# Second half of the tokens laid out turned by the loader, scaled by roots spread over all partitions

## The chip, the cores and the metric

The kernel runs on one core of one Trainium2 chip. The metric is device time of the whole program in microseconds (us); lower is better. The core has a matrix engine (TensorE, PE in the profile), three elementwise engines (VectorE, DVE; ScalarE, ACT; GpSimd, POOL), and SyncE (SP), which here issues almost all DMAs. Every engine runs its own instructions strictly in the order in which they are written, and waits on semaphores for the others.

## The reference

One decoder layer over 2048 tokens of width 1024. The change lies in its first step, the norm and the combined projection:

```python
def rmsnorm(x, g):
    xf = x.astype(jnp.float32)
    y = xf * lax.rsqrt(jnp.mean(xf * xf, axis=-1, keepdims=True) + EPS)
    return (y * g.astype(jnp.float32)).astype(x.dtype)
...
    nx = rmsnorm(h, attn_norm_g[l])
    proj = jnp.einsum('bsd,dp->bsp', nx, w_in[l])
    gq, gk, gv, gr, glow, dq, dk_, dv_ = jnp.split(proj, split_at, axis=-1)
    ... two attention mixers on the pieces of proj, whose results are joined in `mixed` ...
    h = h + jnp.einsum('bsm,md->bsd', mixed, w_out[l])
    nm = rmsnorm(h, mlp_norm_g[l])
    a = jnp.square(jax.nn.relu(jnp.einsum('bsd,df->bsf', nm, w_ff1[l])))
    h = h + jnp.einsum('bsf,fd->bsd', a, w_ff2[l])
return rmsnorm(h, final_norm_g)
```

## The kernel before

**Numbers and products.** All matrix products are made from float32 values split in a rounded part ("hi") and the rest ("lo"): `mm3` (L131) issues three matmuls, hi·hi, lo·hi and hi·lo, into one PSUM bank. The large products are done by a Strassen-Winograd scheme with seven products in place of eight. So every operand has to exist on the chip as hi and lo: ACT makes the hi part by a copy, DVE the lo part by a subtraction.

**The projections** (L222 to L849) take x turned, features on the partitions and tokens along the row. Tokens 0 to 1023 are handled in a first pass (a product ahead of the groups, then groups g = 0 to 7), tokens 1024 to 2047 in a second (g = 8 to 16). For the second pass the kernel needs four blocks of the turned and normed x in SBUF: S11 and S21 (tokens 1024 to 1535, features 0 to 511 and 512 to 1023, in the buffers `xp` and `bp`), S12 and S22 (tokens 1536 to 2047, in two further buffers). S12 is held less S11. Before the change, `pair(i, step)` makes them while the first pass still runs: per i it loads two tiles of 128 tokens into the two halves of `acc[0]` (`x_load`, L553), squares and sums them on ACT with `xt` as the throw-away output (`square`, L571), takes the root (`root`: a tensor_scalar on DVE, L162, and a power on POOL, L163), scales by root and gain on DVE (`scale`, L577), turns them by eight TensorE transposes a tile (`turned`, L560), and moves the result out of PSUM: three copies on ACT (L603, L604, L607) and one subtraction on DVE (L608).

**What sets the order.** In this stage all five engines are ordered by hand. `on(t, f, ...)` files a step under a tick t; a loop (L837) runs through the ticks, emits a tick's steps in the order in which they were filed, and then one `product` of the running group. A narrow group (128 columns, g = 1 to 6) has 14 ticks of six matmuls with 512 columns; a wide one (g = 7 on) 28 ticks of twelve matmuls with 256 columns. Ticks below are counted from `base[0]`, the start of g = 0: g = 1 starts at tick 28, g = 2 at 42, g = 3 at 56, g = 4 at 70, g = 5 at 84, g = 6 at 98, g = 7 at 112. The products of a group are taken in the order j = 1, 2, 6, 5, 7, 4, 3; in a narrow group each has two ticks.

**What a narrow group does beside its products.** `hi` (ACT, L293) five ticks and `lo` (DVE, L298 or L300) three ticks ahead of their product, two in group 7; `wsum` (L305) sums of weight blocks; `evict` reads a bank two ticks after its product began: L364 (ACT) copies j = 1 into c11, L366 (ACT) copies j = 6 into c12, L368 (ACT) copies j = 7 into c21, and L370 and L373 (DVE) add. j = 1, 6 and 7 are summed in one bank, U, one upon the other, so j = 6 can't start before L364 has read it, nor j = 7 before L366 has. `finish_narrow` splits the four results (ACT L387, DVE L389) and stores them (SP L392, or L383 without a split): c11 at tick 7 of its group, c22 at tick 14, c21 at tick 15, c12 at tick 17, which is tick 3 of the next group. The next group's L364 and L366 overwrite c11 and c12 and have to wait for those stores.

**The bias rows.** `bias_rows` (ticks 46 to 52) makes three rows of 8x384 by small matmuls, copies them to `rbo`, whose third part lies in `xt`, and at tick 52 stores them to DRAM as `rowD` (L536).

Of the kernel before, what the change touches and what calls it, by code (L numbers as in the profile page):

```python
# [10 lines left out]
F32 = mybir.dt.float32  # L11
# [7 lines left out]
D = 1024  # L19
# [87 lines left out]
def emit(tc, a, stop=99):  # L107
# [8 lines left out]
    def ps(tag):  # L116
        return psum.tile([128, 512], F32, name="ps_" + tag, tag=tag, bufs=BANKS[tag])
# [5 lines left out]
    def view(t, shape):  # L123
        n = int(np.prod(shape))
        names = "abcd"[:len(shape)]
        return t[:, :n].rearrange(f"p ({' '.join(names)}) -> p {' '.join(names)}", **dict(zip(names, shape)))
# [19 lines left out]
    one = const.tile([1, 128], F32, name="one")  # L146
    V.memset(one, 1.0)
    gn = const.tile([128, 4], F32, name="gn")
    xt = const.tile([128, 1024], F32, name="xt")
    stats = const.tile([128, 96], F32, name="stats")  # L150
    stat_at = [0]
# [81 lines left out]
    def on(t, f, *args):  # L233
        ticks.setdefault(t, []).append((f, args))
# [284 lines left out]
                    on(B + t + dt, gate, g, k, step)  # L519

    rb, oh = bp[:33, :8], view(bp[:33, 8:], (3, 384))
    rbo = [bp[:8, 1160:1544], bp[:8, 1544:1928], xt[:8, :384]]

    def bias_load():
        SP.dma_start(rb[:32], a["rel_bias"])
# [26 lines left out]
    def x_load(t, dst):  # L552
        SP.dma_start(dst, token_rows(x2, t, D))  # L553

    def turned(xt):
        out = []
        for q in range(2):
            pv = view(ps("d"), (4, 128))
            for k in range(4):
                T.transpose(pv[:, k, :], xt[:, (4 * q + k) * 128:(4 * q + k + 1) * 128], ident)  # L560
            out.append(pv)
        return out

    def parts(j, i):
        return [v[:, :, i * 128:i * 128 + 128] for v in TB[j]]

# [2 lines left out]
    def square(key, src, junk):  # L569
        R[key] = stat()  # L570
        A.activation(junk, src, AF.Square, accum_out=R[key])  # L571

    def root(key):
        R[key] = rstd_of(R[key], D)

    def scale(key, src, cs=slice(0, D)):
        V.scalar_tensor_tensor(src[:, cs], src[:, cs], R[key], gB[:, cs], op0=OP.mult, op1=OP.mult)  # L577
# [4 lines left out]
    def blocks_12_22():  # L582
        if not later_blocks:
            later_blocks.update({n: view(slot(n), (4, 512)) for n in ("s12", "s22")})
        return later_blocks.values()


    def pair(i, step):

        at_ = slice(128 * i, 128 * i + 128)  # L590
        x = [acc[0][:, D * k:D * k + D] for k in range(2)]
        if step < 2:
            x_load(8 + i + 4 * step, x[step])
        elif step < 4:
            square((i, step - 2), x[step - 2], xt)
        elif step < 6:
            root((i, step - 4))
        elif step < 8:
            scale((i, step - 6), x[step - 6])
        elif step < 10:  # L600
            PV[0] = turned(x[step - 8])
        elif step == 10:
            A.activation(S11[:, :, at_], PV[0][0], AF.Copy)  # L603
            A.activation(S21[:, :, at_], PV[0][1], AF.Copy)  # L604
        else:
            S12, S22 = blocks_12_22()
            A.activation(S22[:, :, at_], PV[0][1], AF.Copy)  # L607
            V.tensor_tensor(S12[:, :, at_], PV[0][0], S11[:, :, at_], op=OP.subtract)  # L608

    for i in range(4):  # L610
        for step, dt in enumerate((0, 1, 5, 6, 6, 7, 8, 9, 10, 12, 11, 13)):
            on(base[0] + 51 + 18 * i + dt, pair, i, step)

    def half_sum(n, q):

# [117 lines left out]
    with tc.manual_schedule(engines={X.engine for X in (T, V, A, G, SP)}):  # L733
        A.dma_start(g_row, bass.AP(tensor=a["attn_norm_g"].tensor, offset=a["attn_norm_g"].offset, ap=[[D, 1], [1, D]]))
        x_load(0, xs[0])
        load_dv(0)
        x_load(1, xs[1])
        load_dv(1)
        load_dv(2)
        x_load(2, xs[2])  # L740
        load_dv(3)
        for t in range(3, 8):
            x_load(t, xs[t])
        SP.dma_start(w2b[:16], a["gla_gate_w2"].rearrange("o r k -> (o r) k"))
        SP.dma_start(w2b[16:17], a["gla_gate_b"])
        SP.dma_start(gn, bass.AP(tensor=a["gla_norm_g"].tensor, offset=a["gla_norm_g"].offset, ap=[[1, 128], [128, 4]]))
        V.memset(gT, 1.0)
        warm = open_bank()
        for _ in range(8):
            T.transpose(warm[:, :128], ident, ident)  # L750
        gb = [open_bank() for _ in range(2)]
        for q in range(2):
            T.matmul(gb[q], one, g_row[:, 512 * q:512 * q + 512], start=True, stop=True)
        square(0, xs[0], junk)
        V.tensor_copy(gB[:, :512], gb[0])
        root(0)
        V.tensor_copy(gB[:, 512:], gb[1])
        for cs in (slice(0, 512), slice(512, D)):
            scale(0, xs[0], cs)
        tile_T(0)  # L760
        hi_dv(0)
        lo_dv(0)
        square(1, xs[1], junk)
        tile_hi(0)
        tile_lo(0)
        root(1)
        hi_dv(1)
        tile_keep(0)
        dv_piece(0, 0)
        scale(1, xs[1])  # L770
        lo_dv(1)
        tile_T(1)
        dv_piece(0, 1)
        tile_hi(1)
        tile_lo(1)
        hi_dv(2)
        lo_dv(2)
        square(2, xs[2], junk)
        root(2)
        tile_keep(1)  # L780
        scale(2, xs[2])
        hi_dv(3)
        lo_dv(3)
        dv_piece(1, 0)
        dv_piece(1, 1)
        dv_piece(0, 2)
        dv_piece(1, 2)
        square(3, xs[3], junk)
        root(3)
        tile_T(2)  # L790
        tile_hi(2)
        tile_lo(2)
        tile_keep(2)
        scale(3, xs[3])
        dv_piece(0, 3)
        dv_piece(1, 3)
        square(4, xs[4], junk)
        for m in range(4):
            dv_piece(2, m)
            if m == 0:  # L800
                tile_T(3)
                dv_evict(0)
                dv_evict(1)
            if m == 1:
                tile_hi(3)
                tile_lo(3)
                root(4)
                dv_store(0)
                dv_store(1)
        tile_keep(3)  # L810
        scale(4, xs[4])
        for t in range(3, 8):
            n = t + 1
            on(4 * t, dv_evict, t - 1)
            on(4 * t + 2, dv_store, t - 1)
            if n < 8:
                on(4 * t + 1, tile_T, n)
                on(4 * t + 2, tile_hi, n)
                on(4 * t + 2, tile_lo, n)
                on(4 * t + 3, tile_keep, n)  # L820
                on(4 * t + 4, sums_G, n)
                for k, j in enumerate((5, 6)):
                    on(4 * t + 5, part_hi, j, n - 4, halves(n)[k])
                    on(4 * t + 6, part_lo, j, n - 4, halves(n)[k])
            if n < 7:
                on(4 * t + 1, square, n + 1, xs[n + 1], junk)
                on(4 * t + 2, root, n + 1)
                on(4 * t + 3, scale, n + 1, xs[n + 1])
            for m in range(4):
                on(4 * t + m, dv_piece, t, m)  # L830
        on(T0, dv_evict, 7)
        on(T0 + 2, dv_store, 7)
        for i in range(4):
            for k, j in ((0, 7), (1, 4)):
                on(T0 + 1 + 2 * i + k, part_hi, j, i, halves(i)[k])
                on(T0 + 2 + 2 * i + k, part_lo, j, i, halves(i)[k])
        for t in range(12, base[NG] + 10):  # L837
            ops = ticks.pop(t, [])
            for f, args in ops:
                if f is not dv_piece:  # L840
                    f(*args)
            for f, args in ops:
                if f is dv_piece:
                    f(*args)
            if T0 <= t < base[NG]:
                g = max(g for g in range(NG) if base[g] <= t)
                x, i = divmod(t - base[g], length[g])
                product(7 * g + x, i)
        assert not ticks, sorted(ticks)  # L849
# [993 lines left out]
def _order():  # L1843
    r, i = np.divmod(np.arange(128), 8)
    return 16 * i + r
# [28 lines left out]
def build(nc, inputs, stop=99):  # L1874
    arrays, aps = {}, {}
    for name in _INS:
        arrays[name] = np.ascontiguousarray(inputs[name])
    arrays.update(_constants())
    for name, v in arrays.items():
        aps[name] = nc.dram_tensor(name, v.shape, mybir.dt.from_np(v.dtype), kind="ExternalInput").ap()  # L1880
    aps["out"] = nc.dram_tensor("out", (1, S, D), F32, kind="ExternalOutput").ap()
    with tile.TileContext(nc, schedule_with_timeline_sim=True) as tc:
        emit(tc, aps, stop)
    return arrays
# [10 lines left out]
```

## Time and profile before

| | us |
|---|---|
| median of 3 timed runs | 2257.23 (2255.97 to 2259.64) |
| the profiled execution, whole | 2256.31 |
| its span, first to last instruction | 2254.5 |
| PE busy | 2229.1, 99% of the span |
| DVE busy | 1605.4, 71% |
| ACT busy | 1164.0, 52% |
| POOL busy | 812.5, 36% |
| granted TensorE clock | 0.998 |
| DMA, mean | 184 GB/s |

The span leaves out 1.8 us around the instructions. Busy time counts what an engine executes, not its waiting. A line of the timeline gives the start, the length, the engine, the source line and operation, output and inputs, shapes, and in brackets how long the engine sat idle before it and what ended that. An entry of the waits reads: who waited, for whom, us in total, times, longest. For DMAs, the time to landing runs from the issue to the completion that others can wait for.

### The profile page before, as it was taken

The page shows a single profiled execution, that of the slowest core. Times are in us where ns is not written, and L with a number is a line of the kernel's source. Part 1 is how long each engine was busy: PE and PEld are TensorE (multiplying, and loading weights), DVE is VectorE, ACT ScalarE, POOL GpSimd, SP SyncE. Part 2 cuts the span into 40 slices and gives each one's busy share as a digit, 9 for nine tenths or more (in the row PEclk, how much of TensorE's full clock was granted, in tenths as well). Part 3 has the DMA queues.
Part 4 walks back from the last instruction along what each step waited for, and adds up shares of the span by engine and source line. Part 5 has one row for each costly group of instructions (what it writes and reads, how often), then busy time and mean ns, then how long its engine had stood idle before and what let it go on. Part 6 is the DMA issues. An engine that isn't in the chain of part 4 may idle for free.

```text
span 2254.5 us, 34335 instructions
## 1 busy us (share of the span) xinstructions
PE 2229.1 (99%) x12324; PEld 1925.5 (85%) x12324; DVE 1605.4 (71%) x2757; ACT 1164.0 (52%) x2088; POOL 812.5 (36%) x802
## 2 busy tenths in 40 slices
PE   9999999999999999999999999999999999999998
PEld 7978998899999998888888887888888888888886
DVE  6866767746766784446677779777776878758897
ACT  6554446435777782234555557555563333323544
POOL 2111000005378766300122235232345645232665
PEclk9999999999999999999999999999999999999999
DMA  7256444757657864777344457444488653454563
GB/s 207 87 179 194 131 137 153 256 177 238 217 194 240 280 208 150 225 243 263 115 150 145 150 187 226 143 146 148 137 273 306 202 169 130 142 168 149 174 219 112
DMA packets 308267, 415.23 MB, mean 184 GB/s; under 512 B 19509, under 2 KB 236126, under 8 KB 302464
## 3 DMA queue, kind: packets, MB, share of 16 engines
q1 hardware_dynamic: 307950, 412.77, 57.1%
q8 instruction: 97, 1.59, 0.3%
q14 instruction: 74, 0.61, 0.1%
q10 hardware_dynamic: 146, 0.27, 0.0%
HBM read 268.48 MB, written 149.20 MB: 185 GB/s over the span
## 4 chain that ended last, share of the span: by engine, by line
PE 91%; DVE 4%; issue 2%; DMA 1%; ACT 1%; POOL 0%; SPq 0%; POOLq 0%; ACTq 0%; DVEq 0%
PE ps_a L132 11%; PE ps_a L133 11%; PE ps_a L134 11%; PE ps_c L132 9%; PE ps_c L134 8%; PE ps_c L133 8%; PE ps_a L1005 5%; PE ps_d L133 4%; PE ps_d L132 4%; PE ps_d L134 4%; PE ps_d L986 3%; PE ps_c L966 2%; PE ps_c L964 2%; PE ps_o L132 2%; PE ps_o L134 2%; PE ps_o L133 2%
## 5 line engine op out<-in xcount | busy, mean ns | idle before, releaser
L1442 ACT ACTIVATE w1comb<-w1raw 128x512 fp32r<-128x512 f32 x224 | 141.4, 633 | 243.3 <-PE ps_a L134 81.8
L1624 ACT ACTIVATE cs<-rs 128x1024 fp32r<-128x1024 f32 x104 | 109.7, 1055 | 218.7 <-PE ps_c L134 127.8
L1447 DVE TENSOR_TENSOR w1comb<-w1raw,w1comb 128x512 fp32r<-128x512 f32 x224 | 175.8, 786 | 27.5 <-ACT w1comb L1442 27.5
L977 ACT ACTIVATE pe<-pe,O 128x256 f32<-128x256 f32 (+1 forms) x384 | 156.2, 454 | 62.2 <-DVE O L976 57.6
L1005 PE MATMUL ps_a<-v,pt 128*128 128x65 f32 x1200 | 179.0, 252 | 0.0
L1005 PEld LDWEIGHTS ps_a<-v,pt 128*128 128x128 f32 x1200 | 173.4, 193 | 0.9
L986 PE MATMUL ps_d<-ident,pe 128*128 128x128 f32 x600 | 158.1, 278 | 0.0
L976 DVE CUSTOM_DVE_ANT_0 pe<-ps_c,nb 128x256 f32<-128x256 f32 (+1 forms) x384 | 126.7, 361 | 41.5 <-PE ps_d L986 16.8
L132 PE MATMUL ps_a<-hb,w1comb 128*128 128x512 f32 x384 | 149.7, 390 | 0.0
L133 PE MATMUL ps_a<-hb,w1comb 128*128 128x512 f32 x384 | 149.5, 389 | 0.0
L134 PE MATMUL ps_a<-hb,w1comb 128*128 128x512 f32 x384 | 149.4, 389 | 0.0
L1666 DVE TENSOR_TENSOR ct<-rt,ct 128x1024 fp32r<-128x1024 f32 x68 | 129.8, 1909 | 18.8 <-ACT ct L1662 18.8
L133 PE MATMUL ps_c<-ct,cs 128*128 128x512 f32 x360 | 140.1, 389 | 0.0
L132 PE MATMUL ps_c<-ct,cs 128*128 128x512 f32 x360 | 140.1, 389 | 0.0
L134 PE MATMUL ps_c<-ct,cs 128*128 128x512 f32 x360 | 140.1, 389 | 0.0
L163 POOL TENSOR_TENSOR stats<-stats,mhalf 128x1 f32<-128x1 f32 (+1 forms) x64 | 50.0, 783 | 242.6 <-DVE stats L162 242.5
L918 POOL CAST qp<-qs 128x512 fp32r<-128x512 f32 x64 | 66.6, 1126 | 180.2 <-DMA srD<-xp 164.1
L1547 POOL TENSOR_TENSOR acc<-acc 128x256 f32<-128x256 f32 x75 | 69.1, 931 | 160.9 <-DVE acc L1547 148.6
L1631 DVE SCALAR_TENSOR_TENSOR cs<-rs,cs 128x1024 fp32r<-128x1024 f32 (+1 forms) x56 | 100.0, 1793 | 29.6 <-ACT cs L1624 29.3
L293 ACT ACTIVATE wcomb<-wraw 128x512 fp32r<-128x512 f32 (+2 forms) x119 | 89.1, 756 | 60.2 <-DVE wraw L305 25.2
L1547 POOL TENSOR_TENSOR xt<-acc,acc 128x256 f32<-128x256 f32 x32 | 28.1, 878 | 226.7 <-ACT acc L1509 210.3
L986 PEld LDWEIGHTS ps_d<-ident,pe 128*128 128x128 f32 x600 | 108.0, 185 | 0.3
(434 smaller groups left out, 7319.4 us busy)
## 6 DMA issues: line engine op xcount, KB each, us to landing
rs<-actD SPq DMA_DIRECT2D x103, 512.0 KB, 3.7
actD<-acc SPq DMA_DIRECT2D x288, 128.0 KB, 2.9
w1raw<-w_ff SPq DMA_DIRECT2D x32, 1024.0 KB, 6.5
rt<-w_ff SPq DMA_DIRECT2D x24, 1024.0 KB, 7.2
k<-kD SPq DMA_DIRECT2D x16, 1024.0 KB, 8.5
rb<-hTD SPq DMA_DIRECT2D x13, 1024.0 KB, 7.6
wraw<-w_in SPq DMA_DIRECT2D x12, 1024.0 KB, 5.3
cmb<-boD SPq DMA_DIRECT2D x16, 528.0 KB, 6.2
```

What stands on the lines that cost most here:

```text
L132: T.matmul(out, sh, mh, start=first, stop=False, skip_group_check=more)
L133: T.matmul(out, sl, mh, start=False, stop=False, skip_group_check=more)
L134: T.matmul(out, sh, ml, start=False, stop=last, skip_group_check=more)
L976: V.tensor_tensor_reduce(p, s, bias, scale=1.0, scalar=BIG, op0=OP.add, op1=OP.min, accum_out=nm)
L977: A.activation(p, p, AF.Exp, bias=nm, scale=-1.0)
L986: T.transpose(pb[:, i * 128:i * 128 + 128], src, ident)
L1005: T.matmul(self.b.opsum[:, n % 4], self.pt[:, i * 128:i * 128 + 128], self.b.v[:, blk, cols], start=first, stop=last)
L1442: A.activation(c[:, 0], v, AF.Copy)
L1447: V.tensor_tensor(c[:, 1], v, c[:, 0].bitcast(F32), op=OP.subtract)
L1624: A.activation(v[:, 0], x, AF.Copy, scale=float(PRODUCTS[ph // 2][2]))
L1631: V.scalar_tensor_tensor(v[:, 1], x, -1.0, v[:, 0].bitcast(F32), op0=OP.mult, op1=OP.subtract)
L1666: V.tensor_tensor(v[:, 1], x, v[:, 0].bitcast(F32), op=OP.subtract)
```

## The change

The host lays out tokens 1024 to 2047 of x a second time, turned, as `x_turned` (features on 128 partitions by 8 by 1024 tokens). The four blocks S11, S21, S12 and S22 are loaded from it, 1 MB each, straight to their places (`load_turned`). The same tokens are still loaded as rows too, one tile every seven ticks (`tile_stats`), for their squares and roots alone. `spread_roots(k)` then makes a bank whose every partition holds the 512 roots of half k: four float32 matmuls, each with the root column of a tile repeated along 128 columns as the stationary operand and the identity as the moving one. `scale_turned` multiplies a 128x512 piece of a block in place by its gain (`gc`, a new constant of 128x8 loaded in the prologue) and by that bank; `less_first` takes S11 from S12. The third bias row moves from `xt` to `bp`.

```diff
+    gc = const.tile([128, 8], F32, name="gc")
...
-    rbo = [bp[:8, 1160:1544], bp[:8, 1544:1928], xt[:8, :384]]
+    rbo = [bp[:8, 1160:1544], bp[:8, 1544:1928], bp[:8, 8:392]]
...
-    def turned(xt):
-        out = []
-        for q in range(2):
-            pv = view(ps("d"), (4, 128))
-            for k in range(4):
-                T.transpose(pv[:, k, :], xt[:, (4 * q + k) * 128:(4 * q + k + 1) * 128], ident)
-            out.append(pv)
-        return out
...
-    def pair(i, step):
-
-        at_ = slice(128 * i, 128 * i + 128)
-        x = [acc[0][:, D * k:D * k + D] for k in range(2)]
-        if step < 2:
-            x_load(8 + i + 4 * step, x[step])
-        elif step < 4:
-            square((i, step - 2), x[step - 2], xt)
-        elif step < 6:
-            root((i, step - 4))
-        elif step < 8:
-            scale((i, step - 6), x[step - 6])
-        elif step < 10:
-            PV[0] = turned(x[step - 8])
-        elif step == 10:
-            A.activation(S11[:, :, at_], PV[0][0], AF.Copy)
-            A.activation(S21[:, :, at_], PV[0][1], AF.Copy)
-        else:
-            S12, S22 = blocks_12_22()
-            A.activation(S22[:, :, at_], PV[0][1], AF.Copy)
-            V.tensor_tensor(S12[:, :, at_], PV[0][0], S11[:, :, at_], op=OP.subtract)
-
-    for i in range(4):
-        for step, dt in enumerate((0, 1, 5, 6, 6, 7, 8, 9, 10, 12, 11, 13)):
-            on(base[0] + 51 + 18 * i + dt, pair, i, step)
+    def tile_stats(n, step):
+
+        x = acc[0][:, D * (n % 2):D * (n % 2) + D]
+        if step == 0:
+            x_load(8 + n, x)
+        elif step == 1:
+            square(8 + n, x, xt)
+        else:
+            root(8 + n)
+
+    rows = {}
+
+    def spread_roots(k):
+
+        rows[k] = ps("d")
+        for i in range(4):
+            T.matmul(rows[k][:, 128 * i:128 * i + 128], R[8 + 4 * k + i].to_broadcast([128, 128]), ident,
+                     start=True, stop=True)
+
+    def later_block(q, k):
+        return (S11, S21)[q] if k == 0 else list(blocks_12_22())[q]
+
+    def load_turned(q, k):
+        SP.dma_start(later_block(q, k), a["x_turned"][:, 4 * q:4 * q + 4, 512 * k:512 * k + 512])
+
+    def scale_turned(q, k, c):
+        v = later_block(q, k)[:, c]
+        V.scalar_tensor_tensor(v, v, gc[:, 4 * q + c:4 * q + c + 1], rows[k], op0=OP.mult, op1=OP.mult)
+
+    def less_first(c):
+        v = later_block(0, 1)[:, c]
+        V.tensor_tensor(v, v, S11[:, c], op=OP.subtract)
+
+    for n in range(8):
+        for step, dt in enumerate((0, 5, 6)):
+            on(base[0] + 51 + 7 * n + dt, tile_stats, n, step)
+    for k, t in ((0, 80), (1, 108)):
+        on(base[0] + t, spread_roots, k)
+        for q in range(2):
+            on(base[0] + (56, 90)[k] + 2 * q, load_turned, q, k)
+            for c in range(4):
+                on(base[0] + t + 1 + 4 * q + c, scale_turned, q, k, c)
+    for c in range(4):
+        on(base[0] + 110 + c, less_first, c)
...
+        SP.dma_start(gc, bass.AP(tensor=a["attn_norm_g"].tensor, offset=a["attn_norm_g"].offset, ap=[[1, 128], [128, 8]]))
...
+    later = np.asarray(inputs["x"]).reshape(NT, 128, CH, 128)[HT:, _order()]
+    arrays["x_turned"] = np.ascontiguousarray(later.transpose(3, 2, 0, 1).reshape(128, CH, 128 * HT))
```

Two places show how the change moves instructions. The first is SP's queue from tick 51 to tick 60, where group 2 (kD) ends and group 3 begins; before:

```order
L553 DMA acc_134<-x 128x1x1024
L271 DMA wraw_120<-w_in 128x8x256
L553 DMA acc_134<-x 128x1x1024
L536 DMA rowD_107<-bp_112 8x384 x2
L536 DMA rowD_107<-xt_77 8x384
L392 DMA kD1_89<-acc_135 256x1x512
L392 DMA kD1_89<-acc_136 256x1x512
L392 DMA kD0_88<-acc_136 256x1x512
L545 DMA rbD2_110<-rowD_107 128x2x384
```

and in the changed kernel, whose lines and buffer numbers stand one higher:

```order
L554 DMA acc_135<-x 128x1x1024
L272 DMA wraw_121<-w_in 128x8x256
L537 DMA rowD_108<-bp_113 8x384 x3
L393 DMA kD1_90<-acc_136 256x1x512
L603 DMA xp_112<-x_turned 128x4x512
L393 DMA kD1_90<-acc_137 256x1x512
L554 DMA acc_135<-x 128x1x1024
L603 DMA bp_113<-x_turned 128x4x512
L393 DMA kD0_89<-acc_137 256x1x512
L546 DMA rbD2_111<-rowD_108 128x2x384
```

The second row tile is now loaded behind two of the group's three stores instead of ahead of the bias rows, and two loads of 1 MB stand among the stores; the last of them, c12 (kD0 from acc_137), has 2.5 MB of loads in front of it.

The second place is DVE's queue from tick 108 to tick 117, where group 6 ends and the first weights of the wide group 7 are split (128x1024); before:

```order
L370 TENSOR_TENSOR acc<-ps_a,acc 128x512
L373 TENSOR_TENSOR acc<-ps_o,acc 128x512
L298 TENSOR_TENSOR wcomb<-wraw,wcomb 128x1024
L305 TENSOR_TENSOR wraw<-wraw 128x4x256
L162 TENSOR_SCALAR stats<-stats 128x1
L373 TENSOR_TENSOR acc<-ps_a,acc 128x512
L305 TENSOR_TENSOR wraw<-wraw 128x4x256
L162 TENSOR_SCALAR stats<-stats 128x1
L577 SCALAR_TENSOR_TENSOR acc<-acc,stats,misc 128x1024
L298 TENSOR_TENSOR wcomb<-wraw,wcomb 128x1024
```

and in the changed kernel, from the second row of these on (L374 is L373 there, L299 is L298, L306 is L305; s_1706 is the buffer of S12, s_1707 of S22):

```order
L374 TENSOR_TENSOR acc<-ps_o,acc 128x512
L299 TENSOR_TENSOR wcomb<-wraw,wcomb 128x1024
L607 SCALAR_TENSOR_TENSOR s_1706<-s_1706,gc,ps_d 128x512
L611 TENSOR_TENSOR s_1706<-s_1706,xp 128x512
L306 TENSOR_TENSOR wraw<-wraw 128x4x256
L607 SCALAR_TENSOR_TENSOR s_1706<-s_1706,gc,ps_d 128x512
L611 TENSOR_TENSOR s_1706<-s_1706,xp 128x512
L374 TENSOR_TENSOR acc<-ps_a,acc 128x512
L306 TENSOR_TENSOR wraw<-wraw 128x4x256
L607 SCALAR_TENSOR_TENSOR s_1706<-s_1706,gc,ps_d 128x512
L611 TENSOR_TENSOR s_1706<-s_1706,xp 128x512
L607 SCALAR_TENSOR_TENSOR s_1707<-s_1707,gc,ps_d 128x512
```

One more L611 follows, and then the second 128x1024 split. Between the eviction of ps_o and that split, two L162 and one L577 have gone, and four L607 and four L611 have come.

## The prediction

> **What bounds the kernel now.** First the page, its busy times and the chain of work that ended last:
>
> ```profile
> PE 2229.1 (99%) x12324; PEld 1925.5 (85%) x12324; DVE 1605.4 (71%) x2757; ACT 1164.0 (52%) x2088; POOL 812.5 (36%) x802
> PE 91%; DVE 4%; issue 2%; DMA 1%; ACT 1%; POOL 0%; SPq 0%; POOLq 0%; ACTq 0%; DVEq 0%
> ```
>
> PE is busy for 99% of the span and is 91% of the chain. So a PE instruction taken away is worth the time for which it holds up the next one, and any other work costs nothing until PE waits for it. The question is which waits PE has in the stage that changes, and which it will get. The waits from 140 to 260 us, the timeline of ACT and PE around the longest, and the merged chain there:
>
> ```profile
> ACT xt L571 <- DMA rowD<-xt: 4.5, 1, 4.5
> ...
> PE ps_a L132 <- ACT acc L364: 2.6, 1, 2.6
> ...
> PE ps_d L560 <- ACT xp L603: 0.2, 1, 0.2
> ...
> 155.31 1.06 ACT L571 ACTIVATE xt<-acc 128x1024 f32<-128x1024 f32 x1 [4.52 <-DMA rowD<-xt]
> ...
> 156.49 0.39 PE L134 MATMUL ps_c<-tb,wcomb 128*128 128x512 f32 x1
> 159.52 0.50 PE L132 MATMUL ps_a<-tb,wcomb 128*128 128x512 f32 x1 [2.65 <-ACT acc L364]
> ...
> 146.53 8.71 DMA rowD<-xt
> ```
>
> PE waits in this stage only there and briefly at the transposes. The first square (L571) writes its throw-away output into xt, which the store of the third bias row still reads; that store was issued at 146.53 and took 8.71 us for 12 KB, since it stood in a queue behind other transfers. ACT stood still for 4.52 us, the copy L364 came late, and PE with it.
>
> **What goes.** Transposes: the PE timeline around three of the eight batches.
>
> ```profile
> 160.79 0.39 PE L134 MATMUL ps_a<-tb,wcomb 128*128 128x512 f32 x1
> 161.02 1.03 PE L560 MATMUL ps_d<-ident,acc 128*128 128x128 f32 x8
> 161.81 0.47 PE L132 MATMUL ps_a<-tb,wcomb 128*128 128x512 f32 x1
> 162.12 0.40 PE L133 MATMUL ps_a<-tb,wcomb 128*128 128x512 f32 x1
> ...
> 164.43 0.39 PE L134 MATMUL ps_a<-tb,wcomb 128*128 128x512 f32 x1
> 165.06 1.14 PE L560 MATMUL ps_d<-ident,acc 128*128 128x128 f32 x8 [0.24 <-ACT xp L603]
> 165.95 0.48 PE L132 MATMUL ps_a<-tb,wcomb 128*128 128x512 f32 x1
> ...
> 240.65 0.29 PE L134 MATMUL ps_c<-wcomb,tb 128*128 128x256 f32 x1
> 240.77 1.03 PE L560 MATMUL ps_d<-ident,acc 128*128 128x128 f32 x8
> 241.56 0.36 PE L132 MATMUL ps_c<-wcomb,tb 128*128 128x256 f32 x1
> ```
>
> Matmuls of 512 columns start 0.23 us apart, those of 256 columns 0.12. From 160.79 to 162.12 there would be two steps, 0.46 us; it is 1.33, so a batch costs 0.87 us. The second batch, which waits for ACT to empty a bank, costs 1.38 by the same count. Seven at 0.87 to 0.94 and this one make 7.6 us. The wait at 159.52: the next matmul was due at 156.49 + 0.23 = 156.72, so 2.8 us. **Gone: 10.4 us.** With them go 12 ACT copies of 0.6 us, eight DVE scalings and four subtractions; ACT has room, so that is worth nothing by itself.
>
> Here a rule speaks for much more. The Trainium skill, "TensorE: Matmul & The Clock Gate", Part 4 on PE-mode transpose, gives about 275 ns for one in a kernel's context and says that transposes don't count as activity for the clock. By it 64 transposes would be 17.6 us. The rows above have eight of them, each some 270 ns long, in 0.79 us, since they overlap, and the clock in this stage is 1.00; the measurement decides.
>
> **What comes on PE.** Two sets of four float32 matmuls, each in two passes: 16 instructions of 128x128. The nearest rows are products of that shape and type in the attention stage:
>
> ```profile
> 570.40 0.44 PE L1165 MATMUL ps_o<-gla 128*128 128x128 f32 x2
> 570.68 0.39 PE L1166 MATMUL ps_o<-gla 128*128 128x128 f32 x2
> 570.90 0.39 PE L1165 MATMUL ps_o<-gla 128*128 128x128 f32 x2
> ```
>
> Two start in 0.22 to 0.28 us, so eight in 0.95, and some 0.08 us in the step back to the products: 1.0 a set, **2.0 us added** (1.8 to 2.5). Each set also needs the fourth root of its half, one power on POOL, two ticks (2.7 us) earlier. The POOL timeline:
>
> ```profile
> 207.86 0.55 POOL L163 TENSOR_TENSOR stats<-stats,mhalf 128x1 f32<-128x1 f32 x1 [9.30 <-DVE stats L162]
> 238.83 2.66 POOL L163 TENSOR_TENSOR stats<-stats,mhalf 128x1 f32<-128x1 f32 x1 [1.24 <-DVE stats L162]
> ```
>
> Mostly 0.55, 2.66 once beside two long DVE operations. Behind the waiting matmul stands PE's whole stream, so a late root costs in full. I take nothing, with 1.5 us as the other end.
>
> **What comes on the DMA queue, at tick 59.** This is the wait that I expect in place of the removed one. c12 of group 2 is stored at tick 59 and overwritten by L366 at tick 62; PE needs L366 done at tick 64 to add j = 7 upon the same bank. The rows are SP's three stores of kD, landings (of c22 at 150.7; of a store at 183.4, with the queue empty; of the 1 MB loads of qs; of a row tile of x at 224, with the queue empty), and, for 140 to 160 us, the traffic in 40 slices, behind the window from 142 to 156 us (span, busy of PE, PEld, DVE, ACT and POOL, clock, DMA share, GB/s):
>
> ```profile
> 150.68 7.57 SPq L392 DMA_DIRECT2D kD<-acc  x3
> DMA to landing us min/median/max: 5.5/5.5/5.5
> DMA to landing us min/median/max: 3.0/3.0/3.0
> qs<-qD SPq DMA_DIRECT2D x8, 1024.0 KB, 5.1
> acc<-x SPq DMA_DIRECT2D x2, 512.0 KB, 4.7
> 142.00:156.00 14.00, 14.00 (x61) 10.90 (x60) 7.33 (x11) 4.33 (x7) 1.29 (x1) 1.00 1.00 280
> GB/s 0 16 106 377 348 361 359 342 209 372 311 246 166 129 176 176 285 365 375 383 229 150 141 225 226 321 315 228 271 393 389 361 160 16 0 0 0 74 385 356
> ```
>
> The queue is already full here (DMA share 1.00 at 280 GB/s), and 12 KB waited 8.71 us in it, so transfers come out in the order in which they go in. Without the stall the c12 store goes out at about 155, behind c22 (150.7), S11, c21, the row tile and S21. With itself that is four of 0.52 MB and two of 1.05 MB, 4.19 MB. From 151.7 (issue and about 1 us) at 280 GB/s this takes 15.0 us and ends at 166.7; at the 390 GB/s of the two best slices it ends near 162.5. By single landings, less 1.7 us for start and end (3.0 for a store of 0.52 MB, which at 390 GB/s takes 1.3), three stores of 1.3, a tile of 3 and two loads of 3.4 make 13.7 and end at 166. L366, a copy of 128x512, adds 0.6 and a signal 0.1. PE is due at tick 64, 24 matmuls after 156.72, at 162.2. So PE waits between 1.0 and 5.2 us; I take **4.0**, since two of the three accounts lie near 4.5. Behind L366 ACT holds the next hi part, the second square and L368, all with room. S21 itself waits for the bias rows to land, earlier than before as a row tile has left the queue ahead of them; behind it on SP stands the c12 store.
>
> By the Trainium skill, "DMA: Bandwidth & Descriptors", the limit to one core's HBM is some 358 GB/s; the same sum by it is 11.7 us, PE would wait 1.9 and the total be 2.1 lower. The window has a mean of 280, with share 1.00.
>
> The later 2 MB (ticks 90 and 92) precede stores that have six ticks and more, and the row tiles in front of the c12 stores at ticks 73 and 87 add some 1.9 us (0.52 MB at 280) to landings with about that room: nothing, at most 0.5 each.
>
> **What comes on DVE, ticks 110 to 116.** PE, then DVE; at the end a group with PSUM input that is like L607, and steps with 512 columns:
>
> ```profile
> 233.74 0.39 PE L132 MATMUL ps_a<-tb,wcomb 128*128 128x512 f32 x1
> 243.32 0.28 PE L134 MATMUL ps_a<-wcomb,tb 128*128 128x256 f32 x1
> ...
> 233.93 0.69 DVE L373 TENSOR_TENSOR acc<-ps_o,acc 128x512 f32<-128x512 f32 x1 [1.40 <-PE ps_o L134]
> 238.67 1.27 DVE L577 SCALAR_TENSOR_TENSOR acc<-acc,stats,misc 128x1024 f32<-128x1024 f32 x1
> 239.86 1.22 DVE L298 TENSOR_TENSOR wcomb<-wraw,wcomb 128x1024 fp32r<-128x1024 f32 x1
> ...
> L455 DVE SCALAR_TENSOR_TENSOR xt<-ps_d,xt x8: 680/691/700, 100.9 to 384.9; 128x512 f32<-128x512 f32 x8
> 219.14 0.68 DVE L608 TENSOR_TENSOR s<-ps_d,xp 128x512 f32<-128x512 f32 x1
> 219.74 0.68 DVE L298 TENSOR_TENSOR wcomb<-wraw,wcomb 128x512 fp32r<-128x512 f32 x1
> ```
>
> DVE starts on tick 110 at 233.93, 0.19 after PE, and has no gap up to the split at 239.86, 5.93 later, which lasts 1.22. PE uses that part at 243.32, 9.58 after 233.74, and 8.70 without the batch at 240.77. One L577 (1.19 to the next) and two L162 (0.07 each) go, 1.3; four L611 at 0.60 and four L607 at 0.66 (0.06 more for the gain from SBUF) come, 5.0. The split ends 0.19 + 5.93 - 1.3 + 5.0 + 1.22 = 11.0 after PE's tick 110, and PE is due at 8.7: **2.4 us** (1 to 3.5). Afterwards four more L607 take the place of an L577 and an L608, and the slack of the following split, about 1 us, holds.
>
> The eight L607 at ticks 81 to 88 replace two L577 and an L608 there; lo parts have three ticks, and DVE went through two L577 in 3.5 us without a wait of PE. Nothing, 1 at most. The gain constant in the prologue (1024 elements) is first used some 170 us later, and only stores stand right behind it: nothing.
>
> **Sum**, against the profiled execution of 2256.31: -10.4 + 2.0 + 4.0 + 2.4 = -2.0. Later stages keep order and waits and shift whole. The median of the timed runs lies 0.9 higher, 2257.2, so **2255.2 us**.
>
> **Rivals.**
> - The store lands in time. The queue reaches 390 GB/s in slices; PE waits 0 to 1 us at tick 64. Only DVE's 2.4 stays: -5.5, **2251.7**. Against it: share 1.00 at 280 now. Chance 0.25.
> - Neither wait comes (DVE starts ahead, its short operations overlap): -8.4, **2248.8**. Against it: DVE has no gap from 233.93 on. Chance 0.07.
> - The transposes were worth 275 ns each in PE's time: 10.0 more saved than in the forecast, **2245.2**. The rows say no: 0.02. It is the rule of the skill's page on TensorE.
> - Slower: the queue doesn't keep up at tick 59, at the rate that a row tile shows alone (0.52 MB in 4.7 - 1.7 us, 175 GB/s). 4.19 MB take 24 us, PE waits 14, and the time is 2257.2 - 8.4 + 14 + 2.4 = **2265**. It decides from about 205 GB/s down, where the wait passes 10.5. Against it: the 280 with such tiles in the mix. Chance 0.08.
>
> **How the numbers follow.** The forecast has 0.58. About 0.2%, 4.5 us, is what a measurement of this kernel can tell from no change: 2252.7 to 2261.7. Faster are the second, third and first rivals, 0.34; slower 0.08; the forecast is the same, 0.58. Its own range is 2252.5 to 2258 (waits of 1 to 5.2 and 1 to 3.5). The full range reaches down to 2249.5, into the case without waits, and up to 2260, with 1.5 for a late root and 1 for the rest.
>
> **What would show it.** No PE wait at L364 near 157, and ACT's first square unhindered; 64 transposes fewer and 16 matmuls of 0.11 us spacing more; in the waits, ACT's c12 copy of group 3 waiting for the DMA of kD, and PE for that copy, once; PE waiting for DVE's split once at the start of group 7. Without the former it is the first rival, with neither the second. Wrong altogether it would be if PE waited at the spread matmuls for POOL, or if roots came late because squares wait for row tiles in the fuller queue.

## The result, and the profile after

The changed kernel takes **2263.17 us** (median of 11 runs, 2258.38 to 2267.32), the kernel before 2257.23 (11 runs, 2255.62 to 2259.64): a ratio of **1.0025, 95% interval 1.0017 to 1.0033**. In a later series the same two stood at 1.0015 (1.0007 to 1.0024). So it is slower, by 0.2%, where 2255.2 us was forecast and 2260.0 was the end of the range. The profiled execution of the changed kernel took 2262.08 us, with a span of 2260.3.

The page, its busy times and the chain that ended last:

```profile
PE 2227.7 (99%) x12276; PEld 1923.9 (85%) x12276; DVE 1606.2 (71%) x2765; ACT 1157.6 (51%) x2076; POOL 808.7 (36%) x802
...
PE 88%; DVE 5%; DMA 3%; issue 2%; ACT 1%; POOL 0%; SPq 0%; POOLq 0%; ACTq 0%; DVEq 0%
```

PE has 48 instructions fewer and is busy for 1.4 us less, and yet the span is longer: the chain now leads for 3% through DMAs, against 1% before. The waits of all engines from 140 to 270 us:

```profile
ACT acc L367 <- DMA kD<-acc: 12.0, 2, 8.8
...
PE ps_a L132 <- ACT acc L367: 6.3, 1, 6.3
```

The wait of ACT's first square for the bias row is gone, as is PE's behind it, and the wait forecast behind the c12 store is there (6.3 us), longer than forecast. (L367 is L366 of before: the diff adds a line above it.) The timeline at that place, SP's queue first, then ACT and PE:

```profile
150.53 0.54 SPq L393 DMA_DIRECT2D kD<-acc  x1
151.19 0.55 SPq L603 DMA_DIRECT2D xp<-x_turned  x1
153.16 0.52 SPq L393 DMA_DIRECT2D kD<-acc  x1
153.73 0.61 SPq L554 DMA_DIRECT2D acc<-x  x1
154.52 1.13 SPq L603 DMA_DIRECT2D bp<-x_turned  x1
155.70 0.93 SPq L393 DMA_DIRECT2D kD<-acc  x1
156.67 0.69 SPq L546 DMA_DIRECT2D rbD<-rowD  x1
...
150.56 1.05 ACT L563 ACTIVATE xt<-acc 128x1024 f32<-128x1024 f32 x1
...
167.36 1.03 ACT L367 ACTIVATE acc<-ps_a 128x512 f32<-128x512 f32 x1 [8.80 <-DMA kD<-acc]
...
161.79 0.39 PE L134 MATMUL ps_a<-tb,wcomb 128*128 128x512 f32 x1
168.44 0.80 PE L132 MATMUL ps_a<-tb,wcomb 128*128 128x512 f32 x1 [6.26 <-ACT acc L367]
169.03 0.63 PE L133 MATMUL ps_a<-tb,wcomb 128*128 128x512 f32 x1
```

The square at 150.56 starts without a wait. The c12 store, issued at 155.70, has landed at about 167.3; the copy lasts 1.03 us, and PE, due at 161.79 + 0.23 = 162.02, starts at 168.44, 6.4 us late. Then something stands there that no part of the forecast has: the matmuls are 0.63 us long instead of 0.39, and the twelve up to 173.00 start up to 0.43 apart instead of 0.23. The windows view shows why, in stretches of 3.41 us (columns: length, busy us of PE, PEld, DVE, ACT and POOL with counts, granted clock, DMA share, GB/s):

```profile
161.88:165.29 3.41, 0.29 (x2) 0.00 (x0) 0.00 (x0) 0.00 (x0) 0.00 (x0) 1.00 1.04 381
165.29:168.71 3.42, 0.27 (x1) 0.28 (x2) 0.00 (x0) 1.35 (x3) 0.00 (x0) 0.50 1.02 356
168.71:172.12 3.41, 3.41 (x9) 2.64 (x10) 0.75 (x2) 1.65 (x4) 2.02 (x2) 0.50 0.15 44
172.12:175.53 3.41, 3.41 (x17) 2.78 (x16) 1.25 (x2) 1.65 (x3) 0.16 (x1) 1.00 0.87 292
...
243.80:247.21 3.41, 1.19 (x10) 1.19 (x11) 3.41 (x5) 3.21 (x4) 0.00 (x0) 1.00 0.40 78
247.21:250.63 3.42, 3.42 (x19) 3.42 (x18) 2.25 (x4) 0.00 (x0) 0.00 (x0) 0.50 0.02 5
```

The granted clock falls to 0.50 at 165.29, inside the first wait, and stays there for two stretches, one of them with PE at work; behind the second wait it is 0.50 for one. The second wait, at tick 116, PE and then DVE:

```profile
243.49 0.28 PE L133 MATMUL ps_a<-wcomb,tb 128*128 128x256 f32 x1
246.02 0.39 PE L134 MATMUL ps_a<-wcomb,tb 128*128 128x256 f32 x1 [2.25 <-DVE wcomb L299]
...
244.15 0.68 DVE L611 TENSOR_TENSOR s<-s,xp 128x512 f32<-128x512 f32 x1
244.75 1.22 DVE L299 TENSOR_TENSOR wcomb<-wraw,wcomb 128x1024 fp32r<-128x1024 f32 x1
```

PE was due at 243.61 and comes at 246.02: 2.4 us. The split starts only behind the last subtraction (L611).

The starts of the same products in the two traces, after minus before, carry the account:

| product | before | after | difference |
|---|---|---|---|
| behind the removed wait | 159.52 | 156.57 | -2.95 |
| one product behind the store's wait | 170.15 | 173.00 | +2.85 |
| ahead of the late split | 243.08 | 243.37 | +0.29 |
| where the clock is full again | 247.31 | 250.73 | +3.42 |
| the kernel's last product | 2246.91 | 2252.90 | +5.99 |

### The profile page after: what moved, and what is told of

Read it like the earlier page. It is cut to its first block, busy times and chain, and to the rows that moved or that the text cites. A ratio compares the mean times of both kernels' runs of the same rounds, so it can differ in the third digit from the quotient of the medians.

```text
span 2260.3 us, 34224 instructions
## 1 busy us (share of the span) xinstructions
PE 2227.7 (99%) x12276; PEld 1923.9 (85%) x12276; DVE 1606.2 (71%) x2765; ACT 1157.6 (51%) x2076; POOL 808.7 (36%) x802
## 3 DMA queue, kind: packets, MB, share of 16 engines
q8 instruction: 96, 1.57, 0.3%
## 4 chain that ended last, share of the span: by engine, by line
PE 88%; DVE 5%; DMA 3%; issue 2%; ACT 1%; POOL 0%; SPq 0%; POOLq 0%; ACTq 0%; DVEq 0%
PE ps_a L132 10%; PE ps_a L134 10%; PE ps_a L133 10%; PE ps_c L132 8%; PE ps_c L134 8%; PE ps_c L133 8%; PE ps_a L1017 5%; PE ps_d L132 4%; PE ps_d L133 4%; PE ps_d L134 4%; PE ps_d L998 3%; PE ps_c L978 2%; PE ps_c L976 2%; PE ps_o L132 2%; PE ps_o L134 2%
## 5 line engine op out<-in xcount | busy, mean ns | idle before, releaser
L998 PE MATMUL ps_d<-ident,pe 128*128 128x128 f32 x600 | 158.2, 278 | 0.0
L1678 DVE TENSOR_TENSOR ct<-rt,ct 128x1024 fp32r<-128x1024 f32 x68 | 136.0, 2000 | 17.6 <-ACT ct L1674 17.6
L164 POOL TENSOR_TENSOR stats<-stats,mhalf 128x1 f32<-128x1 f32 (+1 forms) x64 | 49.3, 772 | 248.1 <-DVE stats L163 248.0
L1643 DVE SCALAR_TENSOR_TENSOR cs<-rs,cs 128x1024 fp32r<-128x1024 f32 (+1 forms) x56 | 92.6, 1660 | 30.3 <-ACT cs L1636 30.0
```

Of the source, the lines that this page charges most:

```text
L998: T.transpose(pb[:, i * 128:i * 128 + 128], src, ident)
L1678: V.tensor_tensor(v[:, 1], x, v[:, 0].bitcast(F32), op=OP.subtract)
```

## The experiments

Each run is compared with runs of the kernel before on its own chip. The changed kernel stood at 1.0025 and 1.0015 in its two series; a run's gain on it is the distance from these two, and only the last of the fillings ran on one chip with it. Ticks are those of group 0 (`base[0]` plus the number).

**The two loads of x_turned behind the store.**

```diff
-            on(base[0] + (56, 90)[k] + 2 * q, load_turned, q, k)
+            on(base[0] + (62, 90)[k] + 2 * q, load_turned, q, k)
```

> The changed kernel with its two loads of x_turned for tokens 1024 to 1535 issued at ticks 62 and 64 instead of 56 and 58, behind the store that the third block's copy waits for; nothing else differs. Theory (the store stands behind 2 MB in the queue, and the idle engine then loses its clock): the wait of 6.3 us before the product at 168 us goes, and with it the half clock of 165.3 to 172.1 us, which cost 1.5 to 1.8 us. That is 7.5 to 8.5 us less than the changed kernel: about 2255 us, 0.996 to 0.998 of the kernel before, and the PE wait behind the third block's copy is below 1 us. Rival (the megabytes cost the same wherever they stand, since the queue has to carry them): the wait comes back behind the next store or row-tile load, and the time stays at 2261 to 2263 us.

Measured: 2256.21 us, ratio 0.9988 (0.9979 to 0.9997). PE's waits from 140 to 300 us:

```profile
PE ps_a L134 <- DVE wcomb L299: 2.3, 1, 2.3
PE ps_a L132 <- ACT acc L367: 1.0, 1, 1.0
```

The long wait falls to 1.0 us, the clock stays full there, and some 6 to 8 us go, where 7.5 to 8.5 were expected: the same bytes, six ticks later, bring no wait of their own. The rival is out.

**The subtractions behind the split, alone and with the loads.**

```diff
-        on(base[0] + 110 + c, less_first, c)
+        on(base[0] + 120 + 2 * c, less_first, c)
```

> The changed kernel with the four subtractions of less_first at ticks 120, 122, 124 and 126 instead of 110 to 113, so that 2.7 us of VectorE work leave the queue ahead of the split that the product at tick 116 waits for; nothing else differs. Theory (the product waits 2.3 us for a split that VectorE comes to late, and the idle window halves the clock for the next 3.41 us): both go, 2.3 + 1.35 = 3.6 us less than the changed kernel, about 2259.5 us, and the granted clock has no half stretch at 247 us. Rival (VectorE is full in the whole stretch, and the four subtractions make another split late by as much): the wait moves to after 250 us, and the time stays within 1 us of 2263.

> The changed kernel with both moves: the two loads at ticks 62 and 64, and the four subtractions at ticks 120 to 126. Theory (two separate causes, each a wait with a half-clock stretch behind it): the gains add, 8 + 3.6 us, about 2251.5 us, or 0.9975 of the kernel before. Rival (the two waits share their cause, or what is saved early is waited for later): no better than the better of the two alone, 2255 us or more.

Measured: alone 2260.72, ratio 1.0008 (1.0000 to 1.0017); with the loads 2252.89, ratio 0.9975 (0.9965 to 0.9984). In both runs some quarters of S12 are read before S11 is taken from them, so they don't compute the layer and stand here for their times alone; the instructions are as many as before. The wait for the split is gone from both. Alone it took 2 to 4 us less than the changed kernel, together 9 to 11, so the two causes add as far as these times can tell. In the profile of the first the store's wait was 7.3 us, against 6.3 and 6.7 in two executions of the changed kernel: it varies by a microsecond.

**The bias row alone, in the kernel before.**

```diff
-    rbo = [bp[:8, 1160:1544], bp[:8, 1544:1928], xt[:8, :384]]
+    rbo = [bp[:8, 1160:1544], bp[:8, 1544:1928], bp[:8, 8:392]]
```

> The kernel before with one part of the change alone: the third row of bias results lies in bp[:8, 8:392] instead of xt[:8, :384], so that the first square of the row tiles no longer has to wait for the store that reads xt. Theory: the wait of 2.65 to 2.8 us before the product at 159.5 us goes and nothing takes its place, 2254.4 us, 0.9988 of the kernel before. Rival (the next store in the same queue is waited for instead): 2256.5 to 2257.2 us, no change.

Measured: 2255.47, ratio 0.9985 (0.9975 to 0.9994); one PE wait is left from 140 to 300 us:

```profile
PE ps_d L560 <- ACT xp L603: 0.2, 1, 0.2
```

The medians stand 2.6 us apart, so the term of 2.8 us is right by itself, and no wait takes its place.

**One of the two loads behind the store.**

```diff
-            on(base[0] + (56, 90)[k] + 2 * q, load_turned, q, k)
+            on(base[0] + ((56, 62), (90, 92))[k][q], load_turned, q, k)
```

> The changed kernel with only the second of the two loads of x_turned (1 MB into bp) behind the store that the third block's copy waits for, at tick 62; the first stays at tick 56. Theory (the wait is the length of what stands ahead of that store in the queue): 1 MB less at the 286 GB/s that the queue carried there is 3.7 us less, so the wait falls from 6.3 to 2 to 3.5 us and at most one half-clock window of 3.41 us is left of two; 2257.5 to 2260 us. Rival (the store is late for a reason of its own, and either load is enough to bring it about): the wait stays near 6 us and the time near 2263 us.

Measured: 2260.25, ratio 1.0006 (0.9997 to 1.0015). The wait, and two stretches of the clock at the split:

```profile
PE ps_a L132 <- ACT acc L367: 3.5, 1, 3.5
...
242.30:245.71 3.41, 1.57 (x13) 1.57 (x14) 3.41 (x5) 2.82 (x3) 0.00 (x0) 1.00 0.15 57
245.71:249.12 3.41, 3.41 (x19) 3.41 (x18) 2.52 (x5) 0.00 (x0) 0.00 (x0) 0.50 0.02 5
```

With 1 MB less ahead of the store the wait is 2.8 us shorter, and with the other MB gone too (the loads at 62 and 64) another 2.5. The length of the wait is set by what stands ahead of the store. One half-clock stretch is left behind it (167.21 to 170.62), and the time is just above the 2257.5 to 2260 us that the theory gave.

**Filling the waits with transposes.** First only the long one (48 transposes), then both (56 and 16; the edit shown).

```diff
+    def fill(n):
+        p = ps("d")
+        for r in range(n):
+            for q in range(4):
+                T.transpose(p[:, 128 * q:128 * q + 128], ident, ident)
+
+    on(base[0] + 64, fill, 14)
+    on(base[0] + 116, fill, 4)
```

> The changed kernel with 48 transposes of the identity into the bank that is free there, on TensorE just ahead of the product that waits for the third block's copy; their result is not read. 48 times 0.109 us (a batch of eight took 0.87 us) is 5.2 us, less than the wait that they stand in. Theory (the idle TensorE loses its clock for the next windows, which is a cost beside the wait): the product starts when it did, after about 1 us of remaining idle, but there is no half clock at 165 to 172 us; 1.5 to 1.8 us less than the changed kernel, 2261.0 to 2262 us. Rival (the clock falls for another reason than the idle time, or its fall is hidden): the half stretch stays, and the time is 2263 us or more.

> The changed kernel once more, without an edit, so that it stands on the same chip as the run with both fillings. Theory (the two waits and the half-clock windows behind them belong to the kernel and not to one execution): 1.0017 to 1.0033 of the kernel before, a PE wait of 6 to 7.5 us behind the third block's copy, one of 2.3 us behind the split, and a half window wherever one 3.41 us window of the clock is idle for over about 1.8 us, none where it is idle for less. Rival (the half windows were an accident of one execution): no half clock between 160 and 260 us.

> The changed kernel with transposes of the identity, whose result is not read, on TensorE just ahead of both late products: 56 before the one that waits for the third block's copy (56 times 0.109 is 6.1 us, in a wait of 6.4 to 7.3), 16 before the one that waits for the split (1.7 us, in a wait of 2.25). Theory (what the waits cost beyond their length is the half clock behind them): both waits end when they did, there is no half window between 160 and 260 us, and the time is 1.5 to 3.2 us below the changed kernel on the same chip. Rival (the clock costs nothing that the wait does not hide): no difference from the changed kernel.

Measured: the long one filled, 2261.30, ratio 1.0011 (1.0002 to 1.0020). Both filled, 2262.66, 1.0014 (1.0005 to 1.0023), and the changed kernel on the same chip 2262.72, 1.0015 (1.0007 to 1.0024). Windows of the first, then, with both filled, the timeline of PE and of ACT, and PE's waits:

```profile
162.89:166.30 3.41, 3.41 (x34) 3.41 (x33) 0.00 (x0) 0.00 (x0) 0.00 (x0) 1.00 1.05 385
166.30:169.71 3.41, 1.68 (x16) 1.44 (x14) 0.00 (x0) 0.81 (x1) 0.00 (x0) 1.00 0.88 296
169.71:173.13 3.42, 3.15 (x14) 2.62 (x15) 0.75 (x2) 2.29 (x6) 1.48 (x2) 1.00 0.06 23
```

```profile
163.26 6.27 PE L629 MATMUL ps_d<-ident 128*128 128x128 f32 x56
170.24 0.50 PE L132 MATMUL ps_a<-tb,wcomb 128*128 128x512 f32 x1 [0.71 <-ACT acc L367]
170.58 0.40 PE L133 MATMUL ps_a<-tb,wcomb 128*128 128x512 f32 x1
...
189.93 0.60 ACT L367 ACTIVATE acc<-ps_c 128x512 f32<-128x512 f32 x1 [4.30 <-DMA qD<-acc]
```

```profile
PE ps_a L132 <- ACT acc L367: 1.2, 2, 0.7
PE ps_c L132 <- ACT acc L367: 1.0, 1, 1.0
PE ps_a L134 <- DVE wcomb L299: 0.5, 1, 0.5
```

The half clock comes of the idle time: with the waits filled there is none between 160 and 260 us, and in the repeated changed kernel it is there again (166.2 to 173.1 and 248.1 to 251.6). The timed runs say the same: their mean granted clock is 0.995 to 0.997 in the repeated kernel and 0.997 to 0.999 with both filled. But the expected 1.5 to 3.2 us did not come; the two medians are 0.06 us apart, and the rival's "no difference" is what was measured. The first run's gain on the changed kernel, 1 to 3 us by the ratios, can't be told from none.

Where the time went is not settled. In the trace with both filled the products trail those of the changed kernel by 1.24 us ahead of the first place, and by 0.14 behind it (173.14 against 173.00). 16 us on, PE waits 1.0 us for the next copy L367, which waits for a qD store that hasn't landed yet, and at 230 it waits 0.5 us more; at 260 it has won 0.2 us. One account is that PE at half clock comes later to those copies and so doesn't wait. The trace with only the long wait filled doesn't bear it out: there the copy behind the c12 store came 1.0 us later, PE has still won 0.7 us behind the first place, meets no such wait, and has won 2.0 us at 260, 1.5 of them at the split, where the unfilled wait happened to cost no clock (shown at the end). So the slow stretches are real and take 1.6 to 1.8 us each where they stand; of the gain from filling them the traces show 0.2 and 2.0 us, and the times nothing.

**Both edits, with the subtractions in time for their readers** (ticks 117 to 120, loads at 62 and 64), then with **large transfers kept from ahead of every c12 store**.

```diff
-            on(base[0] + (56, 90)[k] + 2 * q, load_turned, q, k)
+            on(base[0] + (66, 90)[k] + 2 * q, load_turned, q, k)
-        on(base[0] + 110 + c, less_first, c)
+        on(base[0] + 118 + c, less_first, c)
-        for step, dt in enumerate((0, 5, 6)):
+        for step, dt in enumerate({1: (3, 8, 9), 3: (2, 5, 6), 5: (2, 5, 6), 7: (2, 5, 6)}.get(n, (0, 5, 6))):
```

> The changed kernel with the two loads at ticks 62 and 64 and the four subtractions of less_first at ticks 117 to 120, behind the late split and ahead of their first reader. Theory (both waits go with their half-clock stretches, and what is left of the change is the removed wait and transposes less the two sets of spread products): as the run with the subtractions at 120 to 126, 2251.5 to 2253 us, 0.9970 to 0.9977 of the kernel before. Rival (the subtractions now hold up the next split or the first split of the turned tokens, which stand right behind them in VectorE's queue): a wait of 1 to 2.5 us at 248 to 256 us, 2254 to 2256.5 us.

> As the run before, with the two loads at ticks 66 and 68, and the row tile that is loaded at tick 58 moved to tick 61 (its square and its root to 66 and 67), so that nothing but two stores stands ahead of the third block's store. Theory (the wait of 1.0 us that was left with the loads at 62 and 64 is the row tile's 0.5 MB ahead of the store): that wait goes too, 1 us less than the run before, 2250.5 to 2252 us. Rival (the rest of the wait is the store's own landing time): no change against the run before.

> The changed kernel with the two loads of x_turned at ticks 66 and 68, the subtractions of less_first at ticks 118 to 121, and the four row tiles that were loaded just ahead of a third block's store (the second, fourth, sixth and eighth) moved 2 or 3 ticks later, behind that store, their squares where they were (the second's 3 ticks later). Theory (each large transfer ahead of such a store shows as a PE wait behind that copy: 1.0 and 0.3 us were left with the loads at 62 and 64, 1.3 with the first tile moved, and 0.6 at the split): these go, no PE wait above 0.4 us is left between 140 and 300 us, and the time is 1 to 2 us below the run with the subtractions in time, 2251 to 2252 us or 0.9966 to 0.9970 of the kernel before. Rival (the stores are late by their own landing time): the waits stay, no change against that run.

Measured: 2252.82, ratio 0.9974 (0.9964 to 0.9983); 2253.08, 0.9975 (0.9966 to 0.9984); 2252.23, **0.9969 (0.9956 to 0.9981)**. PE's waits from 140 to 300 us in the first, and the only one in the third:

```profile
PE ps_a L132 <- ACT acc L367: 1.0, 1, 1.0
PE ps_a L134 <- DVE wcomb L299: 0.6, 1, 0.6
PE ps_c L132 <- ACT acc L367: 0.3, 1, 0.3
```

```profile
PE ps_a L134 <- DVE wcomb L299: 0.7, 1, 0.7
```

With one row tile moved, the first wait went and 1.3 us came at the next such copy; with all four moved both are gone. The traces bear the theory out for these copies; the wait at the split stayed at 0.7 us, where none above 0.4 was expected. The times of the three can't be told apart, so the expected gains of 1 to 2 us from one to the next aren't shown, but each is below both kernels.

**The bias row back in xt, in the first of these three.**

```diff
-    rbo = [bp[:8, 1160:1544], bp[:8, 1544:1928], bp[:8, 8:392]]
+    rbo = [bp[:8, 1160:1544], bp[:8, 1544:1928], xt[:8, :384]]
```

> The changed kernel with the two loads at ticks 62 and 64 and the subtractions at 117 to 120, and the third row of bias results back in xt[:8, :384]. Theory (the removed wait was worth its 2.65 to 2.8 us in this kernel too): ACT's first square waits for the store that reads xt, PE waits 1.8 to 2.8 us behind the next first block's copy, and the wait of 1.0 us behind the third block's copy gets smaller, as that store has the more time; 1.5 to 2.8 us more than the run with the subtractions in time, 2254.5 to 2256 us. Rival (with fewer row tiles ahead of it in the queue the store lands in time anyway): no wait, the same time.

Measured: 2254.91, ratio 0.9979 (0.9968 to 0.9989). ACT's first square, and PE where it waited before:

```profile
153.96 1.06 ACT L563 ACTIVATE xt<-acc 128x1024 f32<-128x1024 f32 x1 [2.13 <-DMA rowD<-xt]
156.06 1.06 ACT L365 ACTIVATE acc<-ps_a 128x512 f32<-128x512 f32 x1
...
157.52 0.39 PE L134 MATMUL ps_c<-tb,wcomb 128*128 128x512 f32 x1
157.74 0.39 PE L132 MATMUL ps_a<-tb,wcomb 128*128 128x512 f32 x1
```

Both expectations missed a part. ACT does wait, 2.1 us instead of 4.5, but PE goes on without a gap. In this kernel one row tile stands ahead of the bias store where before there were two, and one square (L563) ahead of the copy L365 where before there were two (L571, the second at 157.41 for 1.04 us). With a second square the copy would have ended at about 158.2, and PE, due at 157.74, would have waited some 0.4 us. So the spread row tiles remove the wait too, as moving the row does, and moving the row has little left to bring in the changed kernel. The two times don't tell more: their intervals overlap.

## Why the prediction was wrong

**The removed work: right.** Without the two late waits the forecast's own terms, -10.4 and +2.0, give -8.4 us, a ratio of 0.9963. The version with one wait of 0.7 us left measured 0.9969, and 0.9963 lies in its interval. The removed wait shows as 2.95 us in the trace against 2.8. A set of spread matmuls in the changed kernel:

```profile
191.83 0.39 PE L134 MATMUL ps_c<-tb,wcomb 128*128 128x512 f32 x1
192.06 1.05 PE L596 MATMUL ps_d<-ident,stats 128*128 128x128 f32 x8
192.87 0.48 PE L132 MATMUL ps_c<-tb,wcomb 128*128 128x512 f32 x1
193.18 0.39 PE L133 MATMUL ps_c<-tb,wcomb 128*128 128x512 f32 x1
```

From 191.83 to 193.18 it is 1.35 us where two steps would be 0.46: 0.9 a set, forecast 1.0. Neither POOL's powers nor late roots held it up.

**The wait for the split at tick 116: right in size.** 2.4 us forecast, 2.4 us in the trace.

**The wait for the c12 store: the mechanism right, the term mis-sized.** It was put at 4.0 us, with bounds of 1.0 and 5.2; it was 6.4, and the waits give 6.3, 6.7 and 7.3 in three executions with both loads where the change puts them. Three things made it up. The copy behind the store lasts 1.03 us, and 0.6 was taken: 0.4. The trace of the kernel before has 1.10 for this copy:

```profile
163.48 1.10 ACT L366 ACTIVATE acc<-ps_a 128x512 f32<-128x512 f32 x1 [1.31 <-PE ps_a L134]
```

PE was there 0.2 earlier than reckoned. And the store landed at 167.3 where 165.5 was chosen, later than the latest of the three accounts (166.7): 1.8. Two errors stand against each other there. The queue was faster than the 280 GB/s of the sum:

```profile
151.70:167.30 15.60, 10.47 (x47) 8.34 (x45) 6.84 (x11) 4.09 (x6) 1.82 (x2) 0.94 1.02 325
```

15.6 us at 325 GB/s are 5.07 MB, while the store and all ahead of it are 4.19. So transfers did not come out in the order in which they went in, as the prediction put it: some 0.9 MB of what was issued behind the store (the bias rows of 0.39 MB at 156.67, a qD store, a row tile) moved before it was complete. The Trainium skill, "DMA: Bandwidth & Descriptors", "Queues, rings and completion order", says that completion is not first in, first out for one issuing engine, and this trace agrees. In strict order at 325 GB/s the store would have landed at 164.6.

**The clock: left out.** The prediction priced each wait at its length, and the clock that falls with it at nothing. Behind the first, twelve matmuls from 168.44 to 173.00 take 4.56 us where the 0.23 us step makes 2.7: 1.8 us. Behind the second the stretch from 246.02 to 250.73 lasts 4.71 us, and 3.11 in the kernel before (243.32 to 247.31 less a batch of transposes of 0.88): 1.6 us. With -2.0 forecast, +2.4 for the longer wait, +3.4 for the clock and -0.4 for the smaller terms above, the sum is +3.4, which is what the table of starts shows at 250 us.

So two steps failed: the term of the c12 store, 6.4 us where 4.0 stood, and the missing term for the clock, 3.4 us in this trace. By the runs, the waits are shown to be causes: moving the loads and the subtractions takes them away and brings 9 to 11 us. That the clock falls because of the idle time is shown as well, by the fillings. That its 3.4 us stay in the end is not: with both waits filled the time was the same.

**The rest.** The 3.4 us at 250 us agree with the later series, whose medians are 3.6 us apart; in the first they are 5.9 apart, and some 2.5 us of that stay open. The profiled execution of the first loses another 2.6 us from 250 us to the end, 1.5 of it at 1762 to 1775 us. The repeated execution of the same kernel does not lose it: its span is 2257.7, 3.2 above the profile of before. So it doesn't belong to the kernel in every execution, and no part of the change is seen in it. No run settles why a stretch near 1750 us varies by a microsecond or two from one execution to the next.

## What to carry to other kernels

A new load is priced by who stands behind it in its queue: here 2 MB cost 6 to 8 us ahead of a store with a waiter, and no wait six ticks later. Look for the next store with a waiter when moving a load out of the way, since the wait can move there: 1.3 us did. A wait of TensorE of 2 us or more should be priced with a bound above its length, for the clock that may fall behind it, and the gain from filling it not be counted before it is measured.

## What the runs showed of the hardware

How much idle time brings the clock down depends on where the wait lies. The kernel before has a wait of 2.65 us that costs no clock:

```profile
155.13:158.54 3.41, 1.75 (x8) 1.13 (x6) 1.45 (x3) 3.23 (x7) 0.56 (x1) 1.00 0.31 121
158.54:161.95 3.41, 2.43 (x15) 2.12 (x16) 3.38 (x5) 2.29 (x4) 2.87 (x2) 1.00 0.88 238
```

It is spread over two of the 3.41 us stretches. In the changed kernel 2.25 us fall into one and halve the next. With the long wait filled the same wait of 2.25 us happened to lie across two, and the clock stayed full:

```profile
241.39:244.80 3.41, 2.37 (x20) 2.17 (x19) 3.41 (x6) 1.24 (x2) 0.00 (x0) 1.00 0.63 154
244.80:248.22 3.42, 2.21 (x18) 2.21 (x19) 3.42 (x5) 2.19 (x3) 0.00 (x0) 1.00 0.13 38
```

In the changed kernel's trace the half clock begins at 165.29 and again at 247.21 us, 24 times 3.413 us later. Over all profiled executions, counted in stretches that begin where the half clock does, PE busy for 1.68 us or more (idle 1.73 or less) left the next stretch full, and busy for 1.57 or less (idle 1.84 or more) halved it. The one exception is a stretch that was itself at half clock: in the run with the subtractions late, 1.1 us idle there were followed by another. The Trainium skill, "TensorE: Matmul & The Clock Gate", "What's actually happening", gives the free-running stretch of 3413 ns, with which these agree, and its "Why this matters for your kernels" asks for no gap over about 3 us; here gaps of 2.3 us were enough.

PE-mode transposes kept the clock: 6.27 us of nothing else (163.26 above) ran at a granted clock of 1.00 and left it there. The prediction's cited rule, that they don't count as activity, doesn't hold in these runs.
